# One step of a retention and S5 layer on one core: a hand-set table of slots moved for the rotation, the masked scores' product, the sample's states and the gate's transfers

## The chip, the cores and the metric

The kernel runs on one core of a Trainium2 chip. The metric is the device time of one execution in microseconds (us), as the median of several executions. Besides these, one execution was recorded by the hardware profiler; all rows in this document are from such profiled executions, and times in them count from the first instruction (the start of the span).

## The reference

One layer is computed for 2048 new frames of one stream (the prompt) and for 16 frames of each of 8 running streams (the sample, 128 rows together), each row 1024 wide:

```
hn   = rmsnorm(x);  q, k, v, g_ret, u, g_ssm = split(hn @ w_in)      # 1024 x 3072
q, k = rotary(q), rotary(k);  S_t = gamma S_{t-1} + k_t v_t^T        # 4 heads of 128
o    = rmsnorm(q_t S_t) * silu(g_ret)
h    = scan of the diagonal complex state (32 groups x 64);  y = Re(C h) + D u
z    = gelu(y);  z = z * sigmoid(z @ w_glu + b) * silu(g_ssm)
out  = rmsnorm(x + concat[o, z] @ w_out)
```

The retention states and the S5 states after the last frame are outputs too. The retention is done by blocks: the masked scores of a block times v, plus q times the state carried in, and the state moved on by k^T v.

## The kernel before

The rows are 17 tiles of 128: 16 of the prompt and one (tile 16) of the sample. Every product of full accuracy is three float16 products on TensorE, since each operand is kept as a high and a low half.

**Slots.** The order of the work is written by hand. A list, `stream`, has 968 slots, and each is a few TensorE products of one of the large projections: slots 0 to 167 the S5 input u, 168 to 303 head 0 (17 tiles of 8 slots), 304 to 495 the S5 gate, 496 to 903 heads 1 to 3 (136 slots each), 904 to 967 the GLU. Everything else is hung on a slot by `hook(slot, function)` and is issued right behind that slot's products; hooks on the same slot go in the order in which they were registered. The order of each engine's instructions follows from this list alone: TensorE (PE), VectorE (DVE), ScalarE (ACT), GpSimd (POOL) and the DMA-issuing queue SP each run theirs in that order, and each waits where an operand or a buffer isn't ready. So a hook that is moved by a slot moves all that it issues, on all engines, against everything hung on the slots between. A head's slot is three 128x512 float16 products; the gate's slots 304 to 399 are half as long (256 columns), 400 to 431 three quarters.

**A retention step** (class `Step`, one head and one tile, first slot n; the sample's tile is the tenth of each head) has these hooks:

- `r0` at n+7: DVE scales and rotates the projection in the bank `pj` (`Pm`, `A`, line 720), POOL joins them to `rot` (line 724), ACT takes `vt` and the gate `gg` from the bank (lines 727, 733).
- `r1` at n+15: TensorE transposes `rot` (line 738), ACT evicts it as `qkT` (line 740). `r2` at n+18: the scores (line 751), masked by DVE to `sm` (line 754).
- `r3` at n+23: q times the state (line 773), k times v (line 774), masked scores times v (line 775); DVE makes the new state `Sst`; `stats` then squares the output on ACT (`sj`, line 761), forms the inverse root on POOL (`ss`, lines 132 and 133) and scales on DVE (`on`, line 764).
- `r4` at n+28 splits `on` into `oh` (lines 815, 816), `st` at n+32 stores it from SP (line 819).
- For the sample: `r1s` at n+16 makes the masked q (`qm`), `r3s` at n+22 the output (lines 792, 796), and `states` at n+28 makes four products (`sst`, line 805) in the four PSUM banks `o`, `st`, `sc` and `tr`, which DVE adds to the states `Sb` (line 808). Each of these banks has one buffer: the products of `r3` are in `o` and `st`, the transposes of `r1` in `tr`, the scores of `r2` in `sc`.

**S5** (class `S5`): group g has n = 304 + 34 g. `load_v` (n-18) brings its input `uraw` and matrices, `load_y` (n+3) the matrices `craw`; ACT and DVE split them (`wv`, `U`, `wc`), TensorE makes `vps` at n+5 and `yps` at n+45, both in the two `aux` banks, DVE scans and rotates between (`Vs`, `q`, `dh`, `E`), ACT evicts. `uraw` and `craw` share two buffers by turns.

**Weights.** Each head's weights come as 8 `raw` tiles (`load`, line 183), are squared (`wj`, line 196) for the scale, and split into `w` (lines 188, 189). The gate's results `ub` are stored by `flush_store` (line 685). While head 0 runs, the tables of the S5 part are made (`kps` line 569, `wps` line 584, evictions lines 574 and 586).

**The GLU's** operands are split by `Glu.split` (line 1279), and its gate is multiplied in by POOL (`zg`, line 1272).

## Time and profile before

| | before |
|---|---|
| three executions, us | 944.63, 942.03, 944.43 |
| median, us | 944.43 |
| profiled execution: its own time, us | 949.01 |
| its span, first to last instruction, us | 947.2 |
| mean granted TensorE clock | 0.995 |
| busy us: PE, DVE, ACT, POOL | 916.6, 641.6, 438.2, 334.7 |

The profiled execution took 4.6 us longer than the median, and 1.8 us of its own time lie outside its span. A row of the waits reads: engine, line and result that waited, what it waited for, then the us in total, how many times, and the longest. A row of the timeline reads: start, length, engine, line, operation, result and operands, and in brackets the idle time before it and what ended it. A row of the windows has the stretch, then busy us (and instructions) of PE, of PE's weight loads, of DVE, ACT and POOL, the granted clock, the DMA engines' share and GB/s. PE's weight loads (PEld) run beside its products.

### The profile page before, as it was taken

The numbers are of one execution on the slowest core, as the hardware profiler recorded it, in microseconds if no ns is written. First come the engines' busy times: TensorE is split into PE (matmuls) and PEld (weight loads), VectorE is DVE, ScalarE is ACT, GpSimd is POOL, SyncE is SP. The second block draws the span as 40 slices with busy tenths as digits, with TensorE's granted clock in tenths as the row PEclk, the third lists the DMA queues.
The fourth block names the chain that finished last, engine by engine and source line by source line (L and its number), as shares of the span: only waits on it lengthen the run. The fifth ranks groups of instructions, "written<-read, shape, count | busy, mean of one in ns | idle before, by whom it ended". The sixth has DMA issues, their size and how long they took to land.

```text
span 947.2 us, 15916 instructions
## 1 busy us (share of the span) xinstructions
PE 916.6 (97%) x5382; PEld 551.6 (58%) x5382; DVE 641.6 (68%) x1603; ACT 438.2 (46%) x1137; POOL 334.7 (35%) x624
## 2 busy tenths in 40 slices
PE   7999999999988999999999999999999999999997
PEld 7875445555875555655565555656557854444444
DVE  5689755665778746777787777987567945444444
ACT  6575323343566444545445345454446734333241
POOL 1112334432534424545455445565244320000001
PEclk9999999999999999999999999999999999999999
DMA  9999664311596444222132221374263255445442
GB/s 303 99 205 149 108 133 124 82 48 52 105 128 94 97 87 110 76 65 62 38 107 70 70 61 44 111 251 141 63 211 112 83 126 162 117 111 138 140 112 89
DMA packets 161281, 106.15 MB, mean 112 GB/s; under 512 B 80000, under 2 KB 147120, under 8 KB 160688
## 3 DMA queue, kind: packets, MB, share of 16 engines
q1 hardware_dynamic: 161056, 104.88, 46.0%
q8 instruction: 42, 0.69, 0.3%
q14 instruction: 39, 0.32, 0.1%
q10 hardware_dynamic: 144, 0.26, 0.1%
HBM read 64.69 MB, written 35.96 MB: 106 GB/s over the span
## 4 chain that ended last, share of the span: by engine, by line
PE 79%; DVE 5%; DMA 5%; ACT 4%; issue 3%; POOL 3%; SPq 1%; POOLq 0%; ACTq 0%; DVEq 0%
PE pj L707 11%; PE pj L709 11%; PE pj L708 11%; PE outps L1360 6%; PE outps L1362 6%; PE outps L1361 6%; PE ups L693 4%; PE ups L695 4%; PE ups L694 3%; PE ops L775 2%; PE glps L1289 2%; PE glps L1291 2%; PE glps L1290 2%; DMA raw<-in_w_in_dram 2%; DMA uraw<-ud 1%
## 5 line engine op out<-in xcount | busy, mean ns | idle before, releaser
L724 POOL TENSOR_TENSOR rot<-A,Pm 128x128 f32<-128x128 f32 x136 | 77.4, 588 | 106.5 <-DVE A L720 88.3
L707 PE MATMUL pj<-w,R1a 128*128 128x512 f16 x288 | 109.3, 380 | 0.0
L709 PE MATMUL pj<-w,R1a 128*128 128x512 f16 x288 | 109.1, 379 | 0.0
L708 PE MATMUL pj<-w,R1a 128*128 128x512 f16 x288 | 109.1, 379 | 0.0
L1360 PE MATMUL outps<-w,mh 128*128 128x512 f16 (+1 forms) x280 | 104.4, 373 | 0.0
L1361 PE MATMUL outps<-w,mh 128*128 128x512 f16 (+1 forms) x280 | 104.4, 373 | 0.0
L1362 PE MATMUL outps<-w,mh 128*128 128x512 f16 (+1 forms) x280 | 104.4, 373 | 0.0
L709 PE MATMUL pj<-w,R1b 128*128 128x512 f16 x256 | 97.8, 382 | 0.0
L708 PE MATMUL pj<-w,R1b 128*128 128x512 f16 x256 | 97.7, 382 | 0.0
L707 PE MATMUL pj<-w,R1b 128*128 128x512 f16 x256 | 97.7, 382 | 0.0
L727 ACT ACTIVATE vt<-pj,hv 128x128 f32<-128x128 f32 x68 | 25.0, 368 | 148.6 <-DVE A L720 148.6
L693 PE MATMUL ups<-R1a,w 128*128 128x256 f16 (+1 forms) x256 | 74.0, 289 | 2.8 <-ACT ub L671 1.3
L1371 ACT ACTIVATE res<-xo 128x512 f32<-128x512 f32 (+1 forms) x35 | 21.6, 617 | 116.7 <-DVE xo L1370 68.8
L695 PE MATMUL ups<-R1a,w 128*128 128x256 f16 (+1 forms) x256 | 73.8, 288 | 0.4 <-DVE w L189 0.4
L694 PE MATMUL ups<-R1a,w 128*128 128x256 f16 (+1 forms) x256 | 73.8, 288 | 0.0
L1370 DVE SCALAR_TENSOR_TENSOR xo<-outps,ex,xo 128x512 f32<-128x512 f32 (+1 forms) x35 | 25.6, 733 | 64.3 <-PE outps L1362 64.3
L132 POOL TENSOR_TENSOR ss<-ss,C 128x1 f32<-128x1 f32 x68 | 17.7, 260 | 136.5 <-ACT sj L761 136.4
L761 ACT ACTIVATE sj<-ops 128x128 bf16<-128x128 f32 x68 | 18.8, 276 | 94.6 <-PE ops L775 92.7
L764 DVE SCALAR_TENSOR_TENSOR on<-ops,ss,gg 128x128 f32<-128x128 f32 x68 | 23.7, 349 | 51.0 <-POOL ss L133 51.0
L132 POOL TENSOR_TENSOR fs<-fs,half__73 128x1 f32<-128x1 f32 x16 | 3.1, 191 | 154.3 <-DVE fs L1375 154.3
L189 DVE SCALAR_TENSOR_TENSOR w<-raw,gc,w 128x512 f16<-128x512 f32 x48 | 42.0, 879 | 20.3 <-ACT w L188 20.2
L695 PEld LDWEIGHTS <-w 128*128 128x128 f16 x384 | 37.8, 98 | 22.3 <-DVE w L189 0.7
(350 smaller groups left out, 2352.8 us busy)
## 6 DMA issues: line engine op xcount, KB each, us to landing
raw<-in_w_in_dram SPq DMA_DIRECT2D x48, 256.0 KB
raw<-in_w_out_dram SPq DMA_DIRECT2D x32, 256.0 KB
xo<-in_x_prompt_dram SPq DMA_DIRECT2D x16, 512.0 KB
out_dram<-res SPq DMA_DIRECT2D x16, 512.0 KB
R1a<-in_x_prompt_dram SPq DMA_DIRECT2D x9, 512.0 KB
uraw<-ud SPq DMA_DIRECT2D x32, 140.5 KB
yd<-ysb SPq DMA_DIRECT2D x32, 140.0 KB
R1a<-yd SPq DMA_DIRECT2D x4, 1120.0 KB
```

The lines of the kernel that those rows point to most:

```text
L189: V.scalar_tensor_tensor(d[:, 1, :], self.raw, sc, d[:, 0, :], op0=OP.mult, op1=OP.subtract)
L693: mm(ov, w[:, 0, c], hh, start=k == 0, stop=False)
L694: mm(ov, w[:, 0, c], hl, start=False, stop=False)
L695: mm(ov, w[:, 1, c], hh, start=False, stop=k == NK - 1)
L707: mm(self.pj, hh, w[:, 0, :], start=k == 0, stop=False)
L708: mm(self.pj, hh, w[:, 1, :], start=False, stop=False)
L709: mm(self.pj, hl, w[:, 0, :], start=False, stop=k == NK - 1)
L724: G.tensor_tensor(self.rot[:, :, a, :], A[:, :, a, :], Pm[:, :, 1 - a, :], OP.add if a else OP.subtract)
L1360: mm(p, m[:, k, 0, :], w[:, 0, cw], start=k == 0, stop=False)
L1361: mm(p, m[:, k, 0, :], w[:, 1, cw], start=False, stop=False)
L1362: mm(p, m[:, k, 1, :], w[:, 0, cw], start=False, stop=k == NK - 1)
L1370: V.scalar_tensor_tensor(self.x[:, c], p, icc, self.x[:, c], op0=OP.mult, op1=OP.add)
```

## The change

The change is in ten numbers of the table and three small functions:

- `r0` goes from n+7 to n+8. `r3` keeps q times the state and k times v; the product of masked scores and v, and `stats` with it, become `r3b`, one slot later (n+24). For the sample the output's product with the masked scores, which came first in `r3s`, comes last, in `r3b`, two slots behind. `r1s` is at n+17, `states` at n+30 (before n+28), `r4` of a prompt tile at n+29, `st` at n+36.
- In the gate's stretch, `load_v` is issued at n-28 (before n-18) for all groups but the first, `load_y` at n (before n+3), head 1's weights 12 slots earlier, and a gate store two slots later.
- The GLU's first two operands are split in four pieces instead of two.

```
-            mm(po, self.sm, self.vt, start=t == 0, stop=True)
...
-            self.stats(po)
+            self.po = po
+
+        def r3b(self):
+            mm(self.po, self.sm, self.vt, start=self.t == 0, stop=True)
+            self.stats(self.po)
...
-            mm(po[:, 0:128], self.sm, self.vt, start=True, stop=False)
...
-                    mm(po[r, 0:128], self.qm[:, b, r], Sb[:, 2 * g + b, :], start=False, stop=b == 1)
-            self.stats(po[:, 0:128])
+                    mm(po[r, 0:128], self.qm[:, b, r], Sb[:, 2 * g + b, :], start=b == 0, stop=False)
+            self.po = po[:, 0:128]
...
-                hook(len(stream) + 4, flush_store)
+                hook(len(stream) + (6 if gate else 4), flush_store)
...
-        hook(n + 7, s.r0)
+        hook(n + 8, s.r0)
...
-            hook(n + 28, s.states)
+            hook(n + 24, s.r3b)
+            hook(n + 30, s.states)
...
-        hook(n - 18, q.load_v)
-        hook(n + 3, q.load_y)
+        hook(max(n - 28, SP0 + 1) if g else n - 18, q.load_v)
+        hook(n, q.load_y)
...
-            for c in (slice(0, 2), slice(2, 4)):
+            for c in (slice(0, 1), slice(1, 2), slice(2, 3), slice(3, 4)) if self.t < 2 else (slice(0, 2), slice(2, 4)):
```

DVE at the sample's step of head 1, before (`Sb` are the sample's states, `Vs`, `ysb` and `q` belong to S5 groups, `w` is a weight's low half, `Sst` the next step's state):

```order
L754 SCALAR_TENSOR_TENSOR sm<-scps,C 128x128
L1048 SCALAR_TENSOR_TENSOR Vs<-Rm,dh 128x281
L189 SCALAR_TENSOR_TENSOR w<-raw,gc,w 128x512
L808 SCALAR_TENSOR_TENSOR Sb<-Sb,sst 128x256 x4
L1048 SCALAR_TENSOR_TENSOR Vs<-Rm,dh 128x281
L1091 SCALAR_TENSOR_TENSOR ysb<-gw,ysb 128x560
L1055 TENSOR_TENSOR q_5480<-Vs,E_5185 128x281
L816 SCALAR_TENSOR_TENSOR oh<-on,ex,oh 128x128
L777 SCALAR_TENSOR_TENSOR Sst<-Sst,stps 128x128
```

And DVE at the same place now:

```order
L754 SCALAR_TENSOR_TENSOR sm<-scps,C 128x128
L1052 SCALAR_TENSOR_TENSOR Vs<-Rm,dh 128x281
L189 SCALAR_TENSOR_TENSOR w<-raw,gc,w 128x512
L1052 SCALAR_TENSOR_TENSOR Vs<-Rm,dh 128x281
L1095 SCALAR_TENSOR_TENSOR ysb<-gw,ysb 128x560
L1059 TENSOR_TENSOR q_5467<-Vs,E_5185 128x281
L810 SCALAR_TENSOR_TENSOR Sb<-Sb,sst 128x256 x4
L818 SCALAR_TENSOR_TENSOR oh<-on,ex,oh 128x128
L776 SCALAR_TENSOR_TENSOR Sst<-Sst,stps 128x128
```

The four `Sb` additions now stand behind a scan, a `ysb` and a `q`; head 2 has the same rows in the same order.

PE at the same place now, from the four state products of the sample to the next step's products (`ops`, `stps` and `qkps` are in the banks `o`, `st` and `tr`):

```order
L807 MATMUL sst<-v_5231,rot 128x256 x4
L707 LDWEIGHTS R1b
L707 MATMUL pj<-w,R1b 128x512
L708 LDWEIGHTS R1b
L708 MATMUL pj<-w,R1b 128x512
L709 LDWEIGHTS R1b
L709 MATMUL pj<-w,R1b 128x512
L773 MATMUL ops<-Sst,qkT 128x128
L774 MATMUL stps<-vt,rot 128x128
L738 MATMUL qkps<-ident,rot 128x128 x2
```

One slot of projection lies between them now, where three lay before; and the masked scores' product that stood between `stps` and `qkps` is now behind one more slot.

SP in the gate's stretch, a piece of its rows before:

```order
L946 DMA uraw<-wd 128x256
L948 DMA uraw<-ud 128x1x281 x2
L183 DMA raw<-in_w_in_dram 128x4x128
L685 DMA gd<-ub 1024x1x33
L183 DMA raw<-in_w_in_dram 128x4x128
L819 DMA od<-oh 128x256
L685 DMA gd<-ub 1024x1x33
L183 DMA raw<-in_w_in_dram 128x4x128 x2
L685 DMA gd<-ub 1024x1x33
L954 DMA craw<-wd 128x256
```

And from the same load of `uraw` (group 1) on, now:

```order
L950 DMA uraw<-wd 128x256
L952 DMA uraw<-ud 128x1x281 x2
L183 DMA raw<-in_w_in_dram 128x4x128 x2
L821 DMA od<-oh 128x256
L685 DMA gd<-ub 1024x1x33
L780 DMA out_dram<-Sst 128x128
L183 DMA raw<-in_w_in_dram 128x4x128
L821 DMA od<-oh 128x256
L183 DMA raw<-in_w_in_dram 128x4x128
L685 DMA gd<-ub 1024x1x33
```

Before, a gate store, two weight tiles and the store of head 0's last state stood between group 0's load of `craw` and this load of `uraw`; now one weight tile and one store of `od` stand there, and four weight tiles follow it with two gate stores among them.

## The prediction

> **What bounds the kernel now.** I read the page's busy times first, then the waits of PE in the stretch that the change touches, then windows of the places where those waits stand.

> ```profile
> PE 916.6 (97%) x5382; PEld 551.6 (58%) x5382; DVE 641.6 (68%) x1603; ACT 438.2 (46%) x1137; POOL 334.7 (35%) x624
> ```

> PE is busy 97% of the span, so nothing but PE's idle time, and time in which it runs at a lower clock, can be won: the change takes no product away. The waits of PE between 150 and 720 us (total, times, longest) are what the change can reach:

> ```profile
> PE ops L775 <- DVE sm L754: 4.8, 5, 1.6
> PE scps L751 <- ACT qkT L740: 2.4, 4, 0.8
> PE vps L1023 <- ACT U L961: 2.3, 1, 2.3
> PE yps L1071 <- ACT Vs L1027: 1.9, 1, 1.9
> PE wps L584 <- ACT zf L574: 1.6, 2, 0.9
> PE ups L693 <- ACT ub L671: 1.3, 1, 1.3
> PE sst L805 <- DVE sm L754: 1.1, 1, 1.1
> PE nps L1193 <- DVE Sb L808: 0.5, 1, 0.5
> ```

> Together 15.9 us, the most that could be won beside the clock. Three windows of 25 us (PE, PEld, DVE, ACT, POOL, granted clock, DMA share, GB/s) tell what stands behind PE there:

> ```profile
> 250.00:275.00 25.00, 22.68 (x185) 19.36 (x184) 18.84 (x43) 15.44 (x40) 12.15 (x21) 0.93 0.88 146
> 275.00:300.00 25.00, 21.02 (x157) 15.81 (x156) 22.13 (x48) 15.35 (x30) 11.33 (x17) 1.00 0.77 97
> 450.00:475.00 25.00, 23.41 (x131) 14.16 (x130) 18.68 (x46) 11.64 (x35) 12.10 (x24) 1.00 0.14 38
> ```

> In the gate's stretch (the first two) PE idles 2.32 + 3.98 us, the DMA engines are 77% to 88% busy, and DVE has 9.03 of 50 us left. In a head (the third) the DMA engines hardly run and DVE is the second busiest.

> **Head 0's tables.** The `wps` products wait for ACT's eviction `zf` (line 574), which stands behind head 0's `vt` and `gg`:

> ```profile
> 152.70 0.37 ACT L727 ACTIVATE vt<-pj,hv 128x128 f32<-128x128 f32 x1 [1.83 <-DVE A L720]
> 152.97 0.36 ACT L733 ACTIVATE gg<-pj,gc 128x128 f32<-128x128 f32 x1
> 153.22 0.26 ACT L574 ACTIVATE zf<-kps 64x128 f32<-64x128 f32 x1
> ```

> `vt` itself waited 1.83 us for DVE. With `r0` a slot later the `zf` comes ahead of `vt` and goes as soon as its product is there. The row of waits is 1.6 us, and I take it all: **+1.6** (0 to 1.6; `vt` a slot later has a slot's slack in the bank `pj`, which two buffers give).

> **The gate's stretch.** Three PE waits go back to ACT, and ACT's rows of 240 to 300 us show for what it waited:

> ```profile
> ACT wv L968 <- DMA uraw<-wd: 3.3, 3, 2.2
> ACT U L961 <- DMA uraw<-ud: 3.2, 3, 1.7
> ACT ub L671 <- DMA gd<-ub: 2.5, 1, 2.5
> ```

> All three are transfers: an S5 group's matrices, its inputs, and a gate store whose buffer `ub` wanted back. The change issues `uraw` 10 slots earlier (some 0.33 us each here half of a head's 0.64 below, so 3.2 us against waits of 2.2 and 1.7 at most), `craw` 3 slots, head 1's weights 12. That covers each single wait but the store's: `flush_store` is moved two slots back, which stops it from blocking SP while the `ub` is not written, but lands it later; with four buffers it may then be the next late thing. PE's part is 2.3 + 1.9 + 1.3 = 5.5 us. A clock loss is added:

> ```profile
> 264.00:268.00 4.00, 4.00 (x22) 3.08 (x22) 1.94 (x5) 2.92 (x9) 2.13 (x4) 0.58 1.04 114
> ```

> ```profile
> 263.34 0.39 PE L1071 MATMUL yps<-U,wc 128*128 128x280 f32 x1 [1.86 <-ACT Vs L1027]
> ...
> 295.79 0.39 PE L1023 MATMUL vps<-U,wv 128*128 128x280 f32 x1 [2.30 <-ACT U L961]
> ```

> The granted clock is 0.58 over 4 us directly behind the 1.86 us wait, so 4 x 0.42 = 1.7 us of PE's work were lost, and if that wait goes the loss goes. [...] Not every gap does it: the gap of 2.30 us at 295.79 lies in the window from 275 to 300 us, which keeps 1.00.

> So 5.5 + 1.7 = 7.2 us at most. But DVE works 18.84 + 22.13 = 40.97 of these 50 us; in 50 - 7.2 = 42.8 us it would be 96% busy, and the masks, scans and splits that PE waits for would each come a little late. I keep back 1.2 us for that: **+6.0** (from 2, when only the 2.3 us wait goes, to 7.2).

> **The masked scores' product.** `ops` (line 775) waits for `sm` five times. The longest:

> ```profile
> 714.05 0.39 PE L774 MATMUL stps<-vt,rot 128*128 128x128 f32 x2
> 716.07 0.49 PE L775 MATMUL ops<-vt,sm 128*128 128x128 f32 x2 [1.63 <-DVE sm L754]
> ```

> A slot and the transposes now stand between these two products. Their length is read from the next rows (PE at head 1's sample, which serve again below):

> ```profile
> 442.25 0.38 PE L707 MATMUL pj<-w,R1b 128*128 128x512 f16 x1
> 442.46 0.38 PE L708 MATMUL pj<-w,R1b 128*128 128x512 f16 x1
> 442.68 0.38 PE L709 MATMUL pj<-w,R1b 128*128 128x512 f16 x1
> 442.89 0.38 PE L773 MATMUL ops<-Sst,qkT 128*128 128x128 f32 x2
> 443.12 0.39 PE L774 MATMUL stps<-vt,rot 128*128 128x128 f32 x2
> 443.34 0.39 PE L775 MATMUL ops<-vt,sm 128*128 128x128 f32 x2
> 443.56 0.40 PE L738 MATMUL qkps<-ident,rot 128*128 128x128 f32 x2
> ```

> A slot is 442.89 - 442.25 = 0.64 us and the transposes 0.23, so each wait shrinks by up to 0.87. The other four make 4.8 - 1.63 = 3.2 us, 0.8 each, and vanish; the longest keeps 0.76. That is 3.2 + 0.87 = 4.0. Against it stands `r0`: the rotation and POOL's `rot` are a slot later, and the transposes that need `rot` are reached 0.22 sooner, so `rot` can be late where DVE is busy; I set 0.4 for that. **+3.6** (2.5 to 4.4). The statistics also come a slot later, but `r4` moved with them, so no wait is added; the store `st` four slots later stands further from `oh`, on SP.

> **Scores after the transposes.** `scps` waits 2.4 us for `qkT`; at the gate's start ACT had `sj` just ahead of it:

> ```profile
> 246.78 0.30 ACT L761 ACTIVATE sj<-ops 128x128 bf16<-128x128 f32 x1
> ```

> `sj` now belongs to `r3b`, behind `qkT`, which can come 0.3 us sooner each time: four times 0.3 is 1.2, less 0.6 at the gate's start, where the slots are short and `r0` a slot later is felt: **+0.6** (0 to 1.5).

> **End of head 3.** The sample's `sst` waits 1.1 us for `sm` and the statistics of the S5 output (`nps`) 0.5 for `Sb`; in this stretch too the clock is lowered, right behind these waits:

> ```profile
> 684.00:688.00 4.00, 3.89 (x12) 1.77 (x13) 2.45 (x7) 0.00 (x0) 0.00 (x0) 0.57 0.68 184
> ```

> That is 4 x 0.43 = 1.7 us again. The `sst` products two slots later no longer wait, but then the statistics wait for the same `sm`, about 2 us. Of 1.1 + 0.5 + 1.7 = 3.3 I take **+1.0** (-1 to 3.3).

> The GLU's four pieces cost nothing:

> ```profile
> L1279 DVE SCALAR_TENSOR_TENSOR U<-R1a,ex,U 128x560 f16<-128x560 f32 x16 | 18.0, 1160 | 0.1
> ```

> is the row of a tile's halves; four quarters for two tiles give the same elements, and PE can begin on the first a little sooner (-0.8 to +0.8; were DVE not idle there, the two extra starts would be paid).

> **The sample's states.** Here I expect the loss. `states` writes into the four banks `o`, `st`, `sc`, `tr`, and DVE's `Sb` additions free them. The next tile's `r3` and `r1` use `o`, `st` and `tr` again. Before, three slots lay between; now one. DVE at head 1:

> ```profile
> 440.98 1.10 DVE L189 SCALAR_TENSOR_TENSOR w<-raw,gc,w 128x512 f16<-128x512 f32 x1 [0.43 <-ACT w L188]
> 442.00 1.40 DVE L808 SCALAR_TENSOR_TENSOR Sb<-Sb,sst 128x256 f32<-128x256 f32 x4
> 443.33 0.73 DVE L1048 TENSOR_TENSOR_SCAN Vs<-Rm,dh 128x281 f32<-128x281 f32 x1
> 443.98 0.71 DVE L1091 SCALAR_TENSOR_TENSOR ysb<-gw,ysb 128x560 f32<-128x560 f32 x1
> 444.61 1.03 DVE L1055 TENSOR_TENSOR q<-Vs,E 128x281 f32<-128x281 f32 x1
> ```

> The additions ended at 443.40, and PE came to the transposes, the last user of these banks, at 443.56: 0.16 us to spare. Now `Vs`, `ysb` and `q` are ahead of the additions (443.98 - 443.33 + 0.63 + about 0.96 = 2.2 us), and the `w` ahead of those waits for ACT, whose queue is put back a slot by the output's product (0.7). The additions so end at 443.40 + 2.2 + 0.7 = 446.3. PE, without the masked scores' product, reaches the transposes at 443.56 - 0.22 = 443.34. That is 3.0 us of idle PE, longer than any wait in the rows above, and by the row at 264 I add a half clock, 1.7: **-4.7** for head 1. Head 2 has the same rows in the same order: **-9.4** for both (0, when DVE has time in hand, to 2 x 7.2). Head 0's sample stands among short DVE work: **-0.7** (0 to -2).

> **Sum.** 1.6 + 6.0 + 3.6 + 0.6 + 1.0 - 0.7 - 9.4 = +2.7 us. The profiled execution, 949.0, would become 946.3, its span 947.2 - 2.7 = 944.5; the median, 4.6 lower, 944.4 - 2.7 = **941.7**.

> **Rivals.** (1) *The banks come free in time.* The wait of PE gives DVE time that later waits no longer need, or the additions run sooner than I set: at most 1 us per sample and no lower clock. Then -9.4 becomes -2: +10.1, 934.3. For it: 0.16 us of spare was enough before, and DVE in the third window still has 6 us of 25. Against it: DVE's order is fixed, and nothing of it is put behind the additions. (2) *No lower clock at the samples.* The wait comes, the clock stays, as it did behind the gap of 2.3 us: 2 x 1.7 less, +6.1, 938.3. [...] (3) *Slower: the banks' wait grows.* The additions also wait for `Vs` operands from POOL and for an ACT that runs late; at 5.5 us with two lowered windows (3.4) a sample costs 8.9, two 17.8 in place of 9.4: -5.7, 950.1. The sign turns where a sample costs (2.7 + 9.4) / 2 = 6.05 us. (4) *The transfers are not ahead.* The DMA engines are 88% and 77% busy, and a load that is issued sooner only waits longer in the queue; the gate's gain is then 1, not 6: -2.3, 946.7.

> **How the numbers follow.** My own sum has 0.41, rival (1) 0.24, (2) 0.10, (3) 0.18, (4) 0.07. A difference under 0.3%, 2.8 us, is about what a measurement of this kernel can't tell from none. My sum lies just inside that: of its 0.41 I give 0.19 to faster, 0.20 to the same and 0.02 to slower, since the gate's and the sample's terms each have an error of about 3 us. Faster: 0.19 + 0.24 + 0.10 = 0.53; same: 0.20 + 0.07 = 0.27; slower: 0.02 + 0.18 = 0.20. The range takes in rivals (1), (2) and (4) and the near part of (3): 932.5 to 949.5. My sum's own range is 938 to 946.

> **What would show it.** In the profile after: the rows `wps` from `zf`, `yps` from `Vs` and `ups` from `ub` are gone or under 0.3 us, and the windows 260 to 270 keep the clock at 1.00; the `ops` row falls from 4.8 to about 1; `sj` stands behind `qkT` on ACT. A new row, `ops`, `stps` or `qkps` waiting for DVE's `Sb`, shows twice with about 3 us, at heads 1 and 2, and a clock under 0.7 follows. If that row is missing or under 1 us, the sample's term is wrong and the time is near 934; if the ACT rows for `uraw` keep their 2 us in the gate's stretch, the gate's term is.

## The result, and the profile after

The kernel after takes 951.51 us (median of 4 executions, 951.27 to 951.74), the kernel before 944.11 (median of 4). The ratio is 1.0079, with a 95% interval of 1.0062 to 1.0096: it is slower by 7.4 us, where I had forecast 2.7 us faster, and 951.5 lies above the range.

The profiled execution of after is one of 951.74 us with a span of 949.8, so it is a usual one. The engines' busy times on its page:

```profile
PE 917.8 (97%) x5382; PEld 555.6 (58%) x5382; DVE 642.5 (68%) x1607; ACT 442.1 (47%) x1137; POOL 344.3 (36%) x624
```

The counts of instructions are those of before but for four more on DVE, the GLU's pieces; POOL's and ACT's are busy 9.6 and 3.9 us longer at the same counts. The waits of PE between 140 and 724 us (total, times, longest) answer to those of before:

```profile
PE ops L773 <- DVE Sb L810: 5.5, 3, 2.6
PE qkps L738 <- POOL rot L724: 4.3, 4, 1.4
PE nps L1197 <- DVE sm L754: 2.3, 1, 2.3
PE vps L1027 <- DVE U L967: 1.2, 2, 1.0
PE nps L219 <- DVE sm L754: 1.2, 2, 0.6
PE qkps L738 <- DVE Sb L810: 1.1, 4, 0.3
PE glps L1293 <- ACT gg L733: 0.9, 1, 0.9
```

Hardly a row of before is left. `wps` from `zf` is gone, `ops` from `sm` (4.8) is gone, and `ups` from `ub` and `yps` from `Vs`, which went back to transfers, are down to 0.5 and 0.2. But `ops` and `qkps` now wait for `Sb` (5.5 + 1.1), `qkps` for POOL's `rot` (4.3), and `nps` for `sm` (2.3 + 1.2). In the gate's stretch the windows read:

```profile
250.00:275.00 25.00, 23.74 (x207) 20.81 (x207) 23.00 (x48) 17.28 (x43) 13.55 (x22) 1.00 0.66 122
275.00:300.00 25.00, 23.55 (x172) 17.53 (x172) 24.60 (x56) 16.53 (x35) 12.73 (x20) 1.00 0.62 108
```

PE idles 1.26 + 1.45 us there, where it idled 2.32 + 3.98 in the profile before, the clock is whole, and DVE is busy 24.60 of 25 us in the second window.

At head 1's sample, PE of after:

```profile
437.00 0.39 PE L707 MATMUL pj<-w,R1b 128*128 128x512 f16 x1
437.23 0.38 PE L708 MATMUL pj<-w,R1b 128*128 128x512 f16 x1
437.44 0.38 PE L709 MATMUL pj<-w,R1b 128*128 128x512 f16 x1
440.38 0.49 PE L773 MATMUL ops<-Sst,qkT 128*128 128x128 f32 x2 [2.55 <-DVE Sb L810]
440.70 0.49 PE L774 MATMUL stps<-vt,rot 128*128 128x128 f32 x2
```

and DVE of after at the same place:

```profile
436.65 0.93 DVE L189 SCALAR_TENSOR_TENSOR w<-raw,gc,w 128x512 f16<-128x512 f32 x1 [1.01 <-ACT w L188]
437.67 0.74 DVE L1052 TENSOR_TENSOR_SCAN Vs<-Rm,dh 128x281 f32<-128x281 f32 x1
438.33 0.71 DVE L1095 SCALAR_TENSOR_TENSOR ysb<-gw,ysb 128x560 f32<-128x560 f32 x1
438.96 1.03 DVE L1059 TENSOR_TENSOR q<-Vs,E 128x281 f32<-128x281 f32 x1
439.91 1.40 DVE L810 SCALAR_TENSOR_TENSOR Sb<-Sb,sst 128x256 f32<-128x256 f32 x4
```

PE is done with its one slot at about 437.8 and stands until the first addition is over at about 440.3, since `ops` needs the bank `o` first. In that time DVE is not idle, but the four additions come last of its rows; and it began this piece late, since it had stood 1.01 us for ACT's half of `w` (0.43 before).

### The profile page after: what moved, and what is told of

It is laid out like the page before. It is cut to its first block, busy times and chain, and to the rows that moved or that the text cites. A ratio compares the mean times of both kernels' runs of the same rounds, so it can differ in the third digit from the quotient of the medians.

```text
span 949.8 us, 15926 instructions
## 1 busy us (share of the span) xinstructions
PE 917.8 (97%) x5382; PEld 555.6 (58%) x5382; DVE 642.5 (68%) x1607; ACT 442.1 (47%) x1137; POOL 344.3 (36%) x624
## 4 chain that ended last, share of the span: by engine, by line
PE 77%; DVE 8%; POOL 4%; ACT 4%; issue 3%; DMA 3%; SPq 0%; POOLq 0%; DVEq 0%; ACTq 0%
PE pj L707 10%; PE pj L708 10%; PE pj L709 10%; PE outps L1366 6%; PE outps L1365 6%; PE outps L1364 6%; PE ups L693 4%; PE ups L695 4%; PE ups L694 4%; PE qkps L738 2%; PE glps L1293 2%; PE glps L1295 2%; PE glps L1294 2%; PE ops L784 1%; PE scps L751 1%
## 5 line engine op out<-in xcount | busy, mean ns | idle before, releaser
L707 PE MATMUL pj<-w,R1a 128*128 128x512 f16 x288 | 109.3, 380 | 0.0
L709 PE MATMUL pj<-w,R1a 128*128 128x512 f16 x288 | 109.1, 379 | 0.0
L708 PE MATMUL pj<-w,R1a 128*128 128x512 f16 x288 | 109.1, 379 | 0.0
L727 ACT ACTIVATE vt<-pj,hv 128x128 f32<-128x128 f32 x68 | 25.0, 368 | 162.7 <-DVE A L720 157.9
L707 PE MATMUL pj<-w,R1b 128*128 128x512 f16 x256 | 97.7, 382 | 0.0
L708 PE MATMUL pj<-w,R1b 128*128 128x512 f16 x256 | 97.7, 382 | 0.0
L709 PE MATMUL pj<-w,R1b 128*128 128x512 f16 x256 | 97.6, 381 | 0.0
L693 PE MATMUL ups<-R1a,w 128*128 128x256 f16 (+1 forms) x256 | 74.6, 292 | 1.8 <-ACT w L188 1.0
L740 ACT ACTIVATE qkT<-qkps 128x256 f32<-128x256 f32 x68 | 26.0, 382 | 68.0 <-PE qkps L738 67.9
L189 DVE SCALAR_TENSOR_TENSOR w<-raw,gc,w 128x512 f16<-128x512 f32 x48 | 38.8, 812 | 24.1 <-ACT w L188 24.0
```

The source lines that it names most:

```text
L189: V.scalar_tensor_tensor(d[:, 1, :], self.raw, sc, d[:, 0, :], op0=OP.mult, op1=OP.subtract)
L693: mm(ov, w[:, 0, c], hh, start=k == 0, stop=False)
L707: mm(self.pj, hh, w[:, 0, :], start=k == 0, stop=False)
L708: mm(self.pj, hh, w[:, 1, :], start=False, stop=False)
L709: mm(self.pj, hl, w[:, 0, :], start=False, stop=k == NK - 1)
L740: act(self.qkT, p[:, 0:256].rearrange("p (q n) -> p q n", q=2), AF.Copy)
```

## The experiments

Eleven kernels ran, in three groups (e1 to e4, e5 to e8, e9 to e11); the kernels of a group shared a chip and the runs of the kernel before, whose median was 945.21, 943.88 and 944.18 us in the three. Ratios are to those runs. Where slots are compared, it is by the start of a slot's first product in two profiles.

**e1, the kernel before again**, no edit.

> The kernel before, unchanged, to see how far its one profiled execution (949.0, against a median of 944.1) was a usual one. Theory: the excess of 4.9 us was made of waits and lowered clock that usual executions do not have (two lowered windows are 3.4 of it), so this profile shows about 944 with at most one lowered window between 100 and 900 us, and transfer waits in the gate's stretch of under 6 us. Rival: the same waits and the same two lowered windows stand in every execution, and the excess lies elsewhere, so the PE waits of 250 to 300 us are again 6 us or more with a clock of 0.58 behind the one for Vs.

It took 944.80 us, ratio 1.000 (0.998 to 1.002); the profiled execution took 944.21. Windows of the gate's stretch in e1:

```profile
250.00:275.00 25.00, 21.67 (x189) 18.83 (x188) 20.20 (x44) 16.17 (x40) 11.74 (x20) 1.00 0.83 160
275.00:300.00 25.00, 24.02 (x177) 18.09 (x176) 24.60 (x56) 16.91 (x34) 12.74 (x20) 1.00 0.60 95
```

and its waits of PE there, 240 to 300 us:

```profile
PE ups L693 <- ACT ub L671: 1.6, 2, 1.0
PE yps L1071 <- ACT Vs L1027: 1.4, 1, 1.4
PE vps L1023 <- DVE U L963: 1.0, 1, 1.0
```

Of the rows on which I had built the gate's term, the 2.3 us for ACT's `U` is not there, the 1.9 is 1.4, and the clock is 1.00 instead of 0.93. DVE in the second window is at 24.60 of 25 us already, as it is in the kernel after. The first profile of before was an unusual execution in the very place that I costed: its slots 304 to 432 took 3.8 us longer than those of e1, of the 4.8 us between the two spans. The theory holds. With e1 as the profile of before, the start of each slot's products in the two kernels tells where the 7.3 us arise (after less e1):

| stretch (slots) | us |
|---|---|
| start and S5 input (0 to 168) | +2.67 |
| head 0 (168 to 304) | -1.87: -3.66 up to slot 256, then +1.80 at its sample |
| gate (304 to 496) | -1.10 |
| head 1 (496 to 640, with the last steps of its last tiles) | +2.62 |
| head 2 (640 to 776) | +4.51 |
| head 3 (776 to 904) | -0.64 |
| GLU (904 on) | +1.15 |

**e2, after with the states back.**

```
-            hook(n + 30, s.states)
+            hook(n + 28, s.states)
```

> The kernel after, with the sample's states back at n+28. Theory (the banks' wait): the PE waits for Sb at heads 1 and 2 (2.55 + 0.27 us each), the one of head 0 (0.7) and the lowered window behind one of them (1.7) go, so 951.5 - 8 = 943 to 945. Rival: the four state products then wait for the bank o, which the later masked scores' product now holds until DVE has scaled the output, and the wait only changes its name: 949 to 952.

It took 945.22 us, ratio 1.001 (0.9995 to 1.0026), so 6.3 us under the kernel after. Its waits of PE, 140 to 724 us:

```profile
PE qkps L738 <- POOL rot L724: 4.9, 6, 1.4
PE sst L807 <- DVE sm L754: 2.6, 2, 1.7
PE vps L1027 <- DVE U L967: 1.2, 2, 1.0
PE nps L219 <- DVE sm L754: 1.2, 2, 0.6
```

`ops` from `Sb` (5.5) is down to 0.3, and no wait of that size has come in its place; the waits for `rot` and `sm` stay. By the medians that one number of the table holds 6.3 of the 7.4 us. The two profiles put it lower: of the 5.5 us between them, 3.9 arise in heads 1 to 3, and 1.7 in the slots up to 168, ahead of all that this edit moves.

**e3, after with the rotation back.**

```
-        hook(n + 8, s.r0)
+        hook(n + 7, s.r0)
```

> The kernel after, with the rotation r0 back at n+7. Theory: the waits of qkps for POOL's rot (4.3 us in four places) come from the rotation's slot and go: 947 to 948.5. Rival: DVE is simply full there, and the work that r0 now precedes (masks sm, statistics) is late in its place, so that the time is within 1 us of 951.5.

It took 959.09 us, ratio 1.0153 (1.0106 to 1.020). The median stands between two pairs, 955.64 and 955.85 us at a mean clock of 0.998, and 962.32 and 962.66 at 0.991; the profile is the one of 962.32. Neither guess holds: it is worse by 7.6 us, and by 4 even in the faster pair. Its waits of PE, 140 to 724 us, show why:

```profile
PE ops L773 <- DVE on L764: 9.4, 6, 2.8
PE ops L773 <- DVE Sb L810: 2.7, 2, 1.5
PE nps L1172 <- DVE sm L754: 2.7, 1, 2.7
PE nps L219 <- DVE sm L754: 2.6, 2, 1.3
```

The waits for `rot` are gone, but `ops` waits for `on`. The statistics are a slot later, so the rotation of the tile after next now stands ahead of `on` on DVE; `on` is what frees the single bank `o`, and the next `r3` stands for it, 9.4 us in six places. So with the later statistics the rotation needs its later slot in heads 1 to 3, where this profile loses 7 to 8 us a head on e1. In head 0 the same order costs nothing: its tiles are 3.4 us shorter than in e1 up to slot 256.

**e4, both back** (states at n+28, rotation at n+7).

> The kernel after, with both the sample's states at n+28 and r0 at n+7. Theory: both gains add, 951.5 - 8 - 3.5 = 940, faster than before. Rival: they overlap (the same DVE rows are late for both), and it is no better than the better of the two alone, 943 to 945.

It took 960.23 us, ratio 1.0159 (1.0124 to 1.0195). The waits for `Sb` at heads 1 and 2 are gone in its profile, but the gain of e2 does not show: the waits of `ops` for `on` are there as in e3, and `yps` now waits 0.85 us for `Vs` in each of the two heads. Neither guess holds. Why the sum is not lower than e3 was not followed further.

**e5, the kernel after again**, no edit.

> The kernel after, unchanged, to see whether its first profile was a usual one: it lost 2.58 us between slots 0 and 16 to a lowered clock at 16 to 22.7 us, in a stretch that the change does not touch. Theory: that is chance, other executions lack it, and they scatter between 947 and 952. Rival: the change causes it, and every execution again shows the clock of 0.993 to 0.994 and 951 to 952.

It took 951.21 us (950.46 to 951.77), ratio 1.0081 (1.0061 to 1.010), and the profile lost its 2.6 us at the start again. So the theory of a mere accident is not borne out; what is known of the start is told in the last section.

**e6, before with the gate's transfers alone.**

```
+                hook(len(stream) + (6 if gate else 4), flush_store)
+        hook(max(n - 28, SP0 + 1) if g else n - 18, q.load_v)
+        hook(n, q.load_y)
+            ld, sq, sc, sp_ = f0 - 4 if i == 3 else f0 + 8, f0 + 20, f0 + 64, [f0 + 78 + 7 * k for k in range(8)]
```

> The kernel before, with only the transfers of the gate's stretch moved (loads, head 1's weights, the gate's stores). Theory from the profiles of the usual kernel before (e1) and of the kernel after: slots 304 to 432 gain only 1.1 to 1.5 us, since new waits for DVE's U (1.0, 0.9) take the place of the transfers': 943.5 to 944.5 beside 945. Rival, the step as predicted: 6.0 us, 939.

It took 943.51 us, ratio 0.9989 (0.9974 to 1.0004): no difference that can be told. Its profile gains 2.2 us on e1 between slots 304 and 432. Windows:

```profile
250.00:275.00 25.00, 24.31 (x213) 21.38 (x212) 23.23 (x50) 17.16 (x43) 13.57 (x21) 1.00 0.70 131
275.00:300.00 25.00, 23.54 (x172) 17.71 (x172) 24.57 (x55) 16.73 (x34) 12.73 (x19) 1.00 0.57 106
```

PE works 2.64 us more in the first window than in e1 (the slots stand 2.5 us later in it, since the start took longer); in the second, where DVE is at 24.57, 0.48 less. Against the first profile of before, slots 304 to 432 are 6.0 us shorter, which is the size of the prediction; but 3.8 of that the kernel before shows by itself in e1.

**e7, head 0 and the gate.** After, with the slots of heads 1 to 3 and of the sample as in before:

```
+        late = s.h == 0
+        hook(n + (8 if late else 7), s.r0)
...
+            hook(n + (24 if late else 23), s.r3b)
...
+            hook(n + 22, s.r3b)
+            hook(n + 28, s.states)
```

> The gate's transfers and the GLU's pieces as in the kernel after, head 0's tiles with the later rotation and masked product, heads 1 to 3 and the sample's states as before. Theory: the parts add by their slots: head 0 gains 3.7 up to slot 256, the gate 1.1, and the losses of heads 1 to 3 (bank wait, rot, nps) are gone: 945 - 4.8 = 940. Rival: head 0's gain is given back at its sample and the gate's start as it was in the kernel after (1.8 of it), and the whole is 942 to 943.

It took 943.17 us, ratio 0.9997 (0.9984 to 1.0011). Heads 1 and 2 stay level with e1. Head 3 gains 1.4 us; that e1 had a lowered clock there and e7 had none is my estimate, and the mean clocks of the two profiled executions (0.997 and 0.994) don't show it. Head 0 gains its 3.66 us up to slot 256, but its sample gives back 2.5: `ops` waits 1.92 us for `sm`, which with a later rotation isn't there when the sample's output follows at once. The rival is nearer.

**e8, e2 with the transposes and scores a slot later too.**

```
-        hook(n + 15, s.r1)
-        hook(n + 18, s.r2)
+        hook(n + 16, s.r1)
+        hook(n + 19, s.r2)
```

> The kernel after with the states at n+28 (as in e2) and, besides, the transposes and the scores one slot later (n+16, n+19). Theory: the waits of qkps for POOL's rot (3.7 us in four places in e2) are the rotation's missing slot; they go, and with the masked product still one slot behind r3 nothing takes their place: 941 to 942. Rival: the scores are then a slot late for the masked product, and the waits for sm (4.8 us in the kernel before) are back: 945 to 947.

It took 945.31 us, ratio 1.0014 (0.9998 to 1.0029), the same as e2. Its waits, 140 to 724 us:

```profile
PE sst L807 <- DVE sm L754: 3.2, 2, 1.7
PE ops L784 <- DVE sm L754: 2.9, 6, 1.2
PE nps L219 <- DVE sm L754: 2.5, 2, 1.2
PE nps L1172 <- DVE sm L754: 1.2, 1, 1.2
```

The waits for `rot` are gone, as the theory says, and the waits for `sm` have come back in `ops` and grown in `nps`, as the rival says. Wherever the steps of this chain stand, PE waits for one of them.

**e9, e7 with head 0's rotation kept at n+7.**

```
-        hook(n + (8 if late else 7), s.r0)
+        hook(n + 7, s.r0)
...
-            hook(n + 22, s.r3b)
+            hook(n + (24 if late else 22), s.r3b)
```

(and the sample's `r1s` and `st` of head 0 as in after).

> The gate's transfers and the GLU's pieces as in the kernel after; in head 0 the masked product and the statistics one slot later but the rotation kept at n+7, states at n+28; heads 1 to 3 as before. Theory: head 0's gain comes from the statistics that no longer stand ahead of the rotation on DVE, not from a later rotation, and the rotation at n+7 spares the wait of 1.9 us at its sample: head 0 gains 3.4, the gate 1.5 to 2.2, and the kernel is 5 us faster than before, 938.5 to 939.5 where before has 944. Rival: without the later rotation the wps products wait for zf again, and it is 2 us faster at most.

It took 941.24 us (937.60 to 942.15), ratio 0.9963 (0.9946 to 0.9980): the only kernel that is faster than before, by 2.9 us. Its profile, of the execution of 938.02 us, runs level with e1 until slot 184, gains 3.2 us in head 0 and 1.5 in the gate's stretch, and keeps them; another 1.6 arise in head 3. The mean clock of the profiled execution is 0.998, that of e1's 0.997; how much of the 1.6 is the clock was not shown. DVE of e1, where the `wps` of the second table wait:

```profile
150.57 0.35 DVE L764 SCALAR_TENSOR_TENSOR on<-ops,ss,gg 128x128 f32<-128x128 f32 x1 [1.24 <-POOL ss L133]
150.84 0.47 DVE L720 SCALAR_TENSOR_TENSOR Pm<-pj,gc,rots 128x256 f32<-128x256 f32 x1
151.23 0.47 DVE L720 SCALAR_TENSOR_TENSOR A<-pj,gc,rots 128x256 f32<-128x256 f32 x1
```

and DVE of e9 at the same slots:

```profile
149.41 0.48 DVE L720 SCALAR_TENSOR_TENSOR Pm<-pj,gc,rots 128x256 f32<-128x256 f32 x1
149.80 0.48 DVE L720 SCALAR_TENSOR_TENSOR A<-pj,gc,rots 128x256 f32<-128x256 f32 x1
...
152.93 0.35 DVE L764 SCALAR_TENSOR_TENSOR on<-ops,ss,gg 128x128 f32<-128x128 f32 x1 [0.93 <-POOL ss L133]
```

In e1 DVE stood 1.24 us for the statistics with the rotation behind it; in e9 the rotation goes 1.43 us sooner, and `vt`, `gg` and `zf` on ACT 0.8 us sooner (`zf` at 151.48, where e1 has 152.25). The mechanism of the theory holds: the wait for `zf` goes without the rotation's later slot. Its time, 938.5 to 939.5, is not met by the median.

**e10, before with the states alone at n+30.**

```
-            hook(n + 28, s.states)
+            hook(n + 30, s.states)
```

> The kernel before, with the sample's states at n+30 alone. Theory (the banks' wait is DVE's order and PE's one slot, whatever the other parts do): PE waits about 2.5 us for Sb in heads 1 and 2, one of the two with a lowered clock in some executions, head 0 under 1: 950 to 952 where before has 944. Rival: the wait in the kernel after needs the masked product's move too (in before the product stands between, and its own waits for sm then absorb it): 945 to 947.

It took 950.88 us, ratio 1.0064 (1.0038 to 1.0091), 6.7 us over the kernel before, with the wait where the theory puts it, if smaller than its 2.5 us (PE, 140 to 724 us):

```profile
PE ops L775 <- DVE sm L754: 3.7, 3, 2.3
PE ops L773 <- DVE Sb L808: 3.6, 2, 1.8
```

The wait is 1.8 us each, a part of it absorbed where PE waited for `sm` before (two such waits of 0.89 us in e1 are gone). Heads 1 and 2 lose 2.8 and 2.7 us on e1, and from slot 904 on, behind the last tile's wait for `sm`, 2.3 us, it loses 1.5 more. The mean clock of the profiled execution is 0.991, that of e1's 0.997, so a part of these losses can be the clock; at which waits it was lowered is not shown here. The rival, 945 to 947, falls.

**e11, before with the rotation, the masked product and what hangs on it moved**, states at n+28, gate and GLU as before.

> The kernel before, with the rotation, the masked product, its statistics, r4 and the stores moved in all heads (the sample's output too), but states at n+28, the gate's transfers and the GLU as before. Theory: head 0 gains 1.8 net; heads 1 to 3 lose 3 to 4 in waits for rot and for the bank that sm is read from, so the part as a whole costs 1.5 to 2.5: 946 where before has 944. Rival, the step as predicted: it gains 3.6 + 1.6 us and ends at 939 to 940.

It took 947.57 us, ratio 1.0034 (1.0019 to 1.0049): 3.4 us slower, a little worse than the theory and far from the step as predicted. Its profile lies 4.5 us over e1, but 2.8 of these arise up to slot 168, ahead of all that was moved; the rest, 1.7, fits the theory (head 0 -1.8, gate +0.3, slots from 496 on +3.3). Its waits, 140 to 724 us:

```profile
PE qkps L738 <- POOL rot L724: 4.7, 5, 1.4
PE sst L807 <- DVE sm L754: 2.6, 2, 1.7
PE nps L219 <- DVE sm L754: 1.2, 2, 0.6
```

Alone, the three parts give +6.7 (states), +3.4 (masked product) and -0.4 (gate): 9.7, against 7.4 together. That is no proof of an overlap: each of these numbers is uncertain by 1.4 to 2.5 us, and the start, which none of the parts touches, differs by up to 2.7 us from profile to profile.

## Why the prediction was wrong, point by point

Term by term, gains counted positive, with e1 as the profile of before (measured by slots; the masked product is e2 less e1, the states are after less e2):

| term | forecast, us | measured, us |
|---|---|---|
| head 0 with its sample | +0.9 | +1.9 |
| gate's stretch | +6.0 | +1.1 |
| masked product, `scps`, end of head 3, GLU | +5.2 | -3.8 |
| sample's states, heads 1 to 3 | -9.4 | -3.9 |
| start | 0 | -2.7 |
| sum (rows rounded) | +2.7 | -7.3 |

Two terms failed, by 4.9 and 9.0 us. The loss by the states was set too high, by 5.5 us (3.1 by the medians of after and e2), so by luck the sum hides a part of these errors.

**The gate's stretch, +6.0 forecast, 1.1 (after) to 2.2 (e6) measured: the first failed step.** The rows were read rightly, but in an execution that was 4.6 us slower than the median, and I carried these 4.6 us over unchanged ("the median, 4.6 lower"). They were to a large part the very waits and the lowered clock that I then counted as gain: in e1 PE idles 4.3 us in that stretch, not 6.3, and at whole clock. A waiting row in the slow execution was counted twice, once as gain and once as offset. Against that execution itself the term was sized well: slots 304 to 432 are 4.9 us shorter in after and 6.0 in e6, of which e1 has 3.8 with no change at all. The transfers did what they were meant to do: in after no wait of ACT for `uraw` or for a store of `ub` stands among those of this stretch. Of what is left most is a wait for DVE (`U`, 1.0 + 0.2 us, and `ub`, 0.8), which is busy 24.60 of 25 us in the second window, as in e1.

**The masked product, +3.6 forecast (+5.2 with `scps` and the end of head 3): the second failed step.** In e11's profile the slots from 496 on lose 3.3 us on e1 in place of that, in e2's 3.8. The mechanism of the gain was right: the 4.8 us of `ops` from `sm` went. What I set at 0.4, the later rotation, measured 4.3: the transposes came 0.22 sooner and `rot` a slot later, and at 476.97 us POOL's `rot` (1.15 us) was late by 1.37. The rotation stands on DVE behind the statistics' `on` there, and `on` had waited 0.71 us for POOL's `ss`; from 470 to 477 us DVE is busy 6.29 of 7. I had named the term and never worked it out for the tiles where DVE is full, though the rows were there. I also missed that `nps` and `sst` stand behind `r3` on PE: once `ops` no longer waits for `sm` ahead of them, they do (0.6 us in `nps` three times; 1.7 us in head 3's `sst` in e2, where it was 1.1), and the last tile's `gg`, a slot later, makes the GLU's first product wait 0.9. At the end of head 3 `nps` waits 2.3 us for `sm`, as forecast (about 2). The wait for `sm` was not removed; other products took it over.

**Head 0, +1.6 forecast, 3.7 measured up to slot 256.** The mechanism came as forecast: on ACT in after `zf` (152.51 us) stands ahead of the next `vt` (155.94) and waits 0.20 us for its own product alone, and the 1.6 us of `wps` are gone. But the later `r0` is not needed for it: e9 keeps `r0` and has 3.4 of the 3.7, since the statistics' `on` no longer stands ahead of the rotation on DVE. And the size was above my end of 1.6, because a row of waits counts only what PE stands idle, and leaves out gaps under 0.15 us. Most of the rest lies in four steps of about 0.35 us, at slots 219, 232, 235 and 248, which no row shows: at slot 219 `wps` starts 0.28 us later behind the product ahead of it in e1 than in e9, of which 0.12 are idle, and at slot 232 `ops` was 0.24 late for `sm`, of which 0.08 are idle. The sample gave back 1.8, not 0.7: the waits for `Sb` are 0.42 + 0.27, as forecast, `qm` a slot later cost 0.51 besides, and 0.6 stand in no row.

**The sample's states, -9.4 forecast: right in mechanism, too large in size.** The wait is 2.55 + 0.27 us where I had 3.0. Against e1 the slots at the sample (590 to 602, 728 to 740) lost 3.35 us in head 1, and 3.35 + 1.68 in head 2. The difference is the clock: it was lowered behind one of the two. Two windows of after:

```profile
441.00:445.00 4.00, 3.73 (x22) 2.19 (x22) 2.01 (x7) 0.75 (x3) 0.74 (x2) 1.00 0.62 150
565.00:569.00 4.00, 4.00 (x14) 2.07 (x14) 1.45 (x5) 0.75 (x3) 0.74 (x2) 0.57 0.74 183
```

So a part of rival (2) was true. Nor is all of these 8.4 us the states' price: in e2, with the states back, the slots at head 1's sample lose 1.0 on e1 as well, and waits that follow are shorter behind the long one. What the later states add is 1.7 us in head 1 and 3.3 in head 2 (after less e2), 2.8 and 2.7 in e10, and 6.3 and 6.7 by the medians of these two pairs. Rival (3), the right sign, came near in its time (950.1) and not by its mechanism: the banks' wait did not grow, the gains failed.

**The end of head 3 and the GLU.** I took +1.0 together with the four pieces; head 3 gained 0.64 (from 684 to 688 us the clock is 1.00 in after and 0.57 in the first profile of before), and the GLU lost 1.15, of which 0.9 is the wait for `gg`. The pieces have no part in it: e7 and e9 have them too, with head 3 as before, and take as long from slot 904 on as e1, to 0.01 us.

**The start, 2.67 us, stood in no step.** The change does not touch it, and yet the four executions of after have a mean clock of 0.993 to 0.994 and those of e5 0.992 to 0.996, where 48 of the 68 executions of before in the three groups have 0.996 to 0.998. A part of that is the lowered clock in head 2 (0.57 from 565 to 569 us). What is known of it is told below; why it struck after so often was not settled.

## What to carry to other kernels

If the profiled execution is slower than the median by more than the effect that is looked for, its waits are not the kernel's usual ones: an excess taken as a constant offset must not also be counted as gain. Where one engine is busy nine tenths of a stretch (DVE 6.29 of 7 us above), a wait for it that is moved away can come back at the next product that needs the same engine (here 4.8 us of `ops` for `sm` went, and 4.3 of `qkps` for `rot` came), so cost the move by that engine's order of rows, not by the wait's row. And before a step is put nearer to the next user of its buffers, count the rows ahead of it on the engine that frees them: here two slots less and three rows more cost 6.7 us (e10).

## What the runs showed of the hardware

The length of a gap alone does not tell whether the clock falls. In after PE stands 2.56 us until 563.77, and the clock falls at 565.43; it stands 2.55 us until 440.38 and 2.34 until 686.13, and the clock stays whole behind both. In before the clock falls behind a gap of 1.86 us (until 263.34) and not behind one of 2.30 (until 295.79). For the two equal waits of after I have an estimate alone, from the distances above: if the clock could change only every 3.413 us, counted from 565.43, the wait from 561.2 to 563.8 us would lie for 1.76 us between two such times (562.0 and 565.4), and the one from 437.8 to 440.4 would be cut at 439.1 into 1.3 and 1.25. Whether idle time counted so decides it was not shown: counted so from 264.66 in before, PE idles 1.90 us from 291.97 to 295.38, in the gap of 2.30, and no lowered clock follows.

**The start of the program.** In after the clock is lowered early, from 15.88 to 22.71 us. Two windows of its start:

```profile
12.00:16.00 4.00, 2.09 (x17) 1.66 (x16) 2.84 (x14) 1.49 (x4) 0.57 (x1) 0.99 0.90 316
16.00:20.00 4.00, 3.22 (x15) 2.00 (x16) 3.87 (x6) 4.00 (x8) 0.02 (x1) 0.50 1.03 410
```

and of e9, at whole clock:

```profile
12.00:16.00 4.00, 2.12 (x18) 1.70 (x16) 2.84 (x14) 1.40 (x4) 0.67 (x1) 1.00 0.96 351
16.00:20.00 4.00, 2.91 (x25) 2.34 (x26) 3.95 (x6) 4.00 (x8) 0.00 (x0) 1.00 1.02 400
```

The same work, nearly the same idle time of PE from 12 to 16 us (1.91 and 1.88), and 2.5 us of difference by slot 16; why the clock fell in one of the two was not shown. The executions of e9 fall into two groups, five of 937.6 to 938.5 us at a mean clock of 0.998 and seven of 941.2 to 942.2 at 0.993 to 0.994; that the start divides them is likely but not shown, since the one kept trace is of the five. The median of e9 therefore holds some 3 us that depend on how many of its executions have the lower clock; that a kernel's own code decides how many was neither shown nor excluded. Executions of the same mean clock can be compared more sharply: at 0.998 e9 takes 937.6 to 938.5 us and before, in the same group, 941.3 to 942.6; e6, which the medians can't tell from before, takes 940.1 and 940.3 against 941.5 to 942.7.
